# A hybrid decoder layer on one core: the last block's up groups regrouped, background sums queued later, one weight kept at each turn of halves

## The chip, the cores and the metric

The kernel runs on one core of a Trainium2 chip. The metric is the device time of one execution in microseconds (us). Five engines work beside each other: TensorE (PE, matrix products; PEld is its weight load), VectorE (DVE, elementwise work), ScalarE (ACT, activations and copies), GpSimd (POOL; here small copies and the issue of stores) and SyncE (SP; here the issue of loads and of the last stores). Each engine takes its own instructions in program order, and waits on semaphores for what others produce.

## The reference

One layer of a decoder in fp32, model width D = 1024, feed-forward width F = 2816, over 2048 prompt positions behind 16 meta tokens, and 8 sample sequences of 8 positions with cached states. Cut to what matters here:

```python
h = rmsnorm(x, norm1_g)
z = h @ w_in                                  # D -> 5D: za, zg, zp, gate_a, gate_b
a = za * sigmoid(zg)
a = causal_dwconv(a, prev_conv, conv_dw)      # width 31, per channel
conv = swish(layernorm(a + conv_b)) @ w_conv_out
pool = multiscale_pool(zp) @ w_pool * pool_scale
x = x + (sigmoid(gate_a) * conv + sigmoid(gate_b) * pool) @ w_out
u = rmsnorm(x, norm2_g) @ w_up                # D -> 2F
u = causal_dwconv(u, prev_ffn, ffn_dw)        # width 3
x = x + (gelu(gate half of u) * value half of u) @ w_down
y = rmsnorm(x, final_g)
```

The outputs are y for prompt and samples, and the new states of the three convolution and pooling branches.

## The kernel before, in words

**Data.** Channels lie on the 128 partitions, positions on the columns. The 2116 columns are worked in three blocks of 704, 704 and 708 (the last one holds the samples). An activation of one block is eight tiles (KC = 8 channel groups) of up to 708 columns; F is 22 tiles (FC). A block's columns are two halves, `FIRST` and `SECOND`, one for each of the two banks of a PSUM tile; there are four such tiles.

**Products.** Every operand is split in a high and a low part (ScalarE copies the high part, VectorE subtracts, L196 and L181), and a product of tiles is three matmuls (`gemm`, L355; the matmul itself is L222). A weight is loaded raw and split at its first use, and its two parts are stored in DRAM (`keep`); later uses load both parts (`wb<-keep`). There are four buffers for split weights and two for raw ones.

**Units.** The work of TensorE is a list of units, written out ahead for all three blocks: a unit is the products of one output tile with its weight, and behind it a post, the work on VectorE and ScalarE that takes the result out of PSUM. `WO` (L1289) is the output projection with the residual add, `FF` (L1342) the feed-forward part, `DN` (L1323) the down projection of one group of F tiles, added into x. `join` mixes the products of several units: they then go one channel tile at a time. Blocks 0 and 2 run `WO` in halves (all eight output tiles for the first half of the columns, then for the second), so that the norm of the first half can run beside the products of the second.

**Feed-forward groups.** In blocks 0 and 1 the 22 F tiles go in groups of 6, 5, 5, 6, in block 2 (`MIXED`) of 6, 6, 5, 5 (`MIX_GROUPS`). A group's down projection follows behind the first up unit of the next group. In block 2 F tiles from 3 on come from `pair` (L991): a value and a gate tile together by a scheme with seven products in place of eight. There x1, the residual, is stored to DRAM behind each group's down projection (`spill`) and loaded ahead of the next (`fetch`), to make room. The last group's down projection runs in halves in block 2, and its first three units are joined (`JOIN`).

**Background tasks.** Norms, the convolution of width 31 (`conv_norm`, L621, thirty taps for each channel tile on VectorE), the first norm of the next block (`norm1_rstd`) and the output norm (`final`, L1109) are generators. They are dripped in between the units: the planner (`Pace`, L72) holds an estimated time for each engine, and as long as VectorE's estimate lies behind TensorE's, `drip` (L1468) steps the first task whose wait is over. A task says what it waits for with `yield at(tile)` (L376), the estimated time at which that tile is ready. So the estimates alone set the order of instructions on every engine; on the chip only semaphores count.

**Sums over channels** need TensorE. `rsums` (L379) is a matmul with a matrix of ones over the accumulator of the convolution's outputs. `rstd_ps` (L387) sums squares by VectorE and ScalarE (`sumsq`), queues matmuls with a column of ones (L400, `ps<-ones,s` in the profile), works out the reciprocal root on VectorE in ten small instructions (`rs` tiles), and spreads it over the partitions with matmuls against an identity (L416, `ps<-cst,rs`). If such a matmul is queued before its accumulator is done, TensorE stands until it is.

**Weights ahead.** `w_loads` (L299) keeps up to LEAD = 4 weights in flight, counted from the oldest unit's; `w_ahead` and `split_upto` set when the raw ones are split. SyncE issues these loads in order, and x loads, fetches and the last block's y stores with them.

Of the kernel before, what the change touches and what calls it, by code (L numbers as in the profile page):

```python
# [14 lines left out]
P = 128  # L15
D = 1024
KC = D // P
F = 2816
FC = F // P
# [32 lines left out]
W_BUFS = 4  # L52
RAW_BUFS = 2
PLAIN = 3
MIX_GROUPS = (6, 6, 5, 5)
MIX_ROOM = 4
F_GROUPS = (6, 5, 5, 6)
LEAD = 4
# [2 lines left out]
AHEAD = 4  # L61
RESERVE = 3
SLACK = 200.0
JOIN = 3
OWN = 4
POOL_ORDER = (1, 0, 3, 2)
MIXED = (NBLK - 1,)
# [66 lines left out]
def trunk(ctx: ExitStack, tc: tile.TileContext, A, O):  # L134
# [238 lines left out]
        return [(o + t * h, o + (t + 1) * h + halo) for t in ts_]  # L373


    def at(ap):  # L376
        return "at", pace.ready(ap)

    def rsums(acc, n):  # L379

# [3 lines left out]
            mm(ps[:, t, : n // k], ones, acc[:, t * (n // k) : (t + 1) * (n // k)], True, True, 4.0)  # L384
        return ps[:, :k, : n // k]

    def rstd_ps(src, n):  # L387

        acc = yield from sumsq(src, n)
        yield at(acc)
        halves = 1 if n <= 512 else 2
        h = n // halves
        cuts = [(t, c) for t in range(halves) for c in [*range(0, h - P + 1, P)] + [h - P] * (h % P > 0)]
        k = len(cuts)
        ps = PSUM()
        for j, (t, c) in enumerate(cuts):
            mm(ps[:, 0, j : j + 1], acc[:, t * h + c : t * h + c + P], ones[:, :1], True, True, 260.0)  # L400
        del acc
        yield at(ps)
        w = mpool.tile([P, 4, 6], F32, tag="rs", name=nm("rs"), bufs=3)
        v, r, m, q = (w[:, i, :k] for i in range(4))
        ts(v, ps[:, 0, :k], EPS, None, ALU.add)
        ts(r.bitcast(I32), v.bitcast(I32), -0.5, MAGIC, ALU.mult, ALU.add)
        tt(m, r, r, ALU.mult)
        stt(m, m, -1.0, v, ALU.mult, ALU.mult)
        ts(q, m, 0.375, 1.25, ALU.mult, ALU.add)
        tt(q, q, m, ALU.mult)  # L410
        stt(r, q, 1.875, r, ALU.add, ALU.mult)
        tt(m, r, r, ALU.mult)
        stt(m, m, -0.5, v, ALU.mult, ALU.mult)
        stt(r, m, 1.5, r, ALU.add, ALU.mult)
        for j, (t, c) in enumerate(cuts):
            mm(ps[:, t, c : c + P], w[:, 1, j : j + 1].to_broadcast([P, P]), cst[:, O_ID : O_ID + P], True, True, 4.0)  # L416
        yield at(ps)
        return ps[:, :halves, :h]

    def rstd_of(src, n):  # L420
        ps = yield from rstd_ps(src, n)
        yield from room(1)
        out = S(n)
        act(wide(out, ps), ps, AF.Copy)
        yield at(out)
        return out
# [68 lines left out]
    def norm1_rstd(b):  # L495
        W = WIDTHS[b]
        yield from room(3)
        xs = [x_load(b, c) for c in range(2)]

        def src(c):  # L500
            x = xs.pop(0)
            if c + 2 < KC:
                xs.append(x_load(b, c + 2))
            yield at(x)
            return x

        R["rstd1", b] = yield from rstd_of(src, W)

    def h_make(b, last):
        while ("rstd1", b) not in R:  # L510
# [110 lines left out]
    def conv_norm(b):  # L621

        W = WIDTHS[b]

        def sums(c):
            if c % 2 == 0:
                yield from conv_pair(b, c)
            yield
            return R["cv", b, c]

        acc = None
        for c in range(KC):
            cv = yield from sums(c)
            if c == 1:
                yield from room(1)
                acc = S(W)
                tt(acc, R["cv", b, 0], cv, ALU.add)
            elif c:
                tt(acc, acc, cv, ALU.add)
        yield at(acc)  # L640
        ps = rsums(acc, W)
        del acc
        yield at(ps)
        yield from room(1)
        mu = S(W)
        act(mu.rearrange("p (a c) -> p a c", a=2), ps, AF.Copy)

        def src(c):
            if c == 0:
                yield at(mu)  # L650
            cv = R["cv", b, c]
            tt(cv, cv, mu, ALU.subtract)
            yield
            return cv

        ps = yield from rstd_ps(src, W)
        for c in range(KC):
            cv = wide(R["cv", b, c], ps)
            tt(cv, cv, ps, ALU.mult)
            R["cvn", b] = c + 1  # L660
            yield
# [127 lines left out]
    def add_post(b, c, ts_, ps, key):  # L789
        x = R["x1", b, c]  # L790
        yield at(x)
        tt(sb(x, b, ts_), sb(x, b, ts_), ps_of(ps, b, ts_), ALU.add)
        if key:
            for t in ts_:
                R[key, b, t] = c + 1
        yield

    def x_part(b, ts_, key):
        c0, c1 = cols(b, ts_)

        def src(c):
            ok = lambda: all(R.get((key, b, t), 0) > c for t in ts_)
            while not ok():
                yield "cond", ok
            x = R["x1", b, c][:, c0:c1]
            yield at(x)
            return x

        return src
# [298 lines left out]

    def final(b, ts_):  # L1109
        c0, c1 = cols(b, ts_)  # L1110
        r = yield from (rstd_ps if b == NBLK - 1 and ts_[-1] == 1 else rstd_of)(x_part(b, ts_, "x2n"), c1 - c0)
        for c in range(KC):
            x = R["x1", b, c][:, c0:c1]
            o = wide(x, r) if len(r.shape) == 3 else x
# [28 lines left out]
    def W(key, src, n=None):  # L1143
        wq.append(Weight(key, src, n or src.shape[1]))
        return len(wq) - 1
# [142 lines left out]

    def WO(b, parts):  # L1289
        mark["WO", b] = len(units)  # L1290
        for ts_ in parts:
            for c in range(KC):
                std_unit(
                    W(("out", c), A["w_out"][c]), lambda: R["m", b], b, ts_,
                    lambda ps, c=c, ts_=ts_: add_post(b, c, ts_, ps, "x1n"), (), wait=c == 0,
                    pre=(lambda c=c: x_again(b, c)) if ts_ == parts[0] else None,
                    drop=("m", b) if ts_ == parts[-1] and c == KC - 1 else None,
                )
                if c == 1 and ts_ == FIRST:
                    join(mark["WO", b])  # L1300
# [21 lines left out]

    def DN(b, f0, f1, parts=(BOTH,)):  # L1323
        first = len(units)
        for ts_ in parts:
            for c in range(KC):
                def after(ps, c=c, ts_=ts_):
                    yield from add_post(b, c, ts_, ps, "x2n" if f1 == FC else None)
                    if f1 < FC and b in MIXED:
                        spill(b, c)  # L1330
                    if c == KC - 1 and ts_[-1] == 1:
                        for f in range(f0, f1):
                            del R["f", b, f]

                std_unit(
                    W(("dn", c, f0, f1), A["w_dn"][c][:, f0 * P : f1 * P]), lambda: [R["f", b, f] for f in range(f0, f1)],
                    b, ts_, after, (), c == 0, pre=(lambda c=c: fetch(b, c)) if b in MIXED and ts_[0] == 0 else None,
                )
                if f1 == FC and c + 1 == JOIN and ts_ == parts[0]:
                    join(first)  # L1340

    def FF(b, parts, last_parts):  # L1342
# [11 lines left out]
        for gs in MIX_GROUPS if b in MIXED else F_GROUPS:  # L1354
            for f in range(f0, f0 + gs):
                if b in MIXED and f >= PLAIN:
                    pair(b, f)
                else:
                    if f > 1:
                        up(b, f, w_up(f), nd + ((("mx", b),) if b in MIXED and f == PLAIN - 1 else ()))  # L1360
                    if f:
                        up(b, FC + f, w_up(FC + f), nd)
                if f == f0 and pend:
                    DN(b, *pend)
                    pend = None
            pend = (f0, f0 + gs)
# [259 lines left out]
```

## Time and profile before

| what | value |
| --- | --- |
| median of 3 runs (lowest to highest) | 2970.05 us (2966.85 to 2970.11) |
| the profiled execution | 2964.97 us, of which the span of the trace 2963.1 us |
| TensorE busy | 2913.6 us, 98% |
| VectorE busy | 2034.2 us, 69% |
| ScalarE, GpSimd busy | 818.3 us (28%), 393.9 us (13%) |
| mean granted clock of TensorE | 0.992 |
| DMA | 660.13 MB, mean 223 GB/s |

In the rows of the profile, a line of the waits view gives who waits for what, the total in us, how often, and the longest; a line of the timeline gives the start, the length, the engine, line and operation with out<-in, the count, and in brackets the idle time just before it and what ended it. In the window rows "(x...)" counts instructions and PEclk is the mean granted clock over the stretch.

### The profile page before, as it was taken

The numbers are of one execution on the slowest core, as the hardware profiler recorded it, in microseconds if no ns is written. First come the engines' busy times: TensorE is split into PE (matmuls) and PEld (weight loads), VectorE is DVE, ScalarE is ACT, GpSimd is POOL, SyncE is SP. The second block draws the span as 40 slices with busy tenths as digits, with TensorE's granted clock in tenths as the row PEclk, the third lists the DMA queues.
The fourth block names the chain that finished last, engine by engine and source line by source line (L and its number), as shares of the span: only waits on it lengthen the run. The fifth ranks groups of instructions, "written<-read, shape, count | busy, mean of one in ns | idle before, by whom it ended". The sixth has DMA issues, their size and how long they took to land.

```text
span 2963.1 us, 44420 instructions
## 1 busy us (share of the span) xinstructions
PE 2913.6 (98%) x17928; PEld 2906.4 (98%) x17928; DVE 2034.2 (69%) x3007; ACT 818.3 (28%) x1238; POOL 393.9 (13%) x752
## 2 busy tenths in 40 slices
PE   7999999999999999999999999999999999999997
PEld 7999999999999999999999999999999999999997
DVE  7998998679997454743498999655672136544645
ACT  5201334333223232522221212223252113221322
POOL 1111210020010101232110000233320010000000
PEclk9999999999999999999999999999999999999999
DMA  7424554955655655798644344799964375788786
GB/s 278 157 83 163 200 204 169 343 211 176 233 178 201 215 209 189 262 337 292 247 153 150 132 139 144 266 317 320 349 230 150 131 277 185 266 281 272 269 292 241
DMA packets 156780, 660.13 MB, mean 223 GB/s; under 512 B 24992, under 2 KB 31264, under 8 KB 114720
## 3 DMA queue, kind: packets, MB, share of 16 engines
q1 hardware_dynamic: 104112, 416.19, 41.6%
q0 software_dynamic: 52464, 241.11, 20.6%
q8 instruction: 141, 2.31, 0.3%
q14 instruction: 63, 0.52, 0.1%
HBM read 433.17 MB, written 224.05 MB: 222 GB/s over the span
## 4 chain that ended last, share of the span: by engine, by line
PE 71%; DVE 12%; issue 10%; DMA 3%; POOL 2%; ACT 1%; SPq 0%; DVEq 0%; POOLq 0%; ACTq 0%
PE ps L222 71%; DVE s L185 7%; DVE s L181 3%; DVE wb L181 2%; POOL keep L216 2%; DMA wb<-keep 1%; DMA raw<-in_w_up 1%; DMA keep<-s 1%; ACT s L196 1%; DMA keep<-wb 0%; ACT wb L196 0%; POOL raw L210 0%; DMA s<-in_x 0%; SPq L205 0%; DVE rs L185 0%
## 5 line engine op out<-in xcount | busy, mean ns | idle before, releaser
L222 PE MATMUL ps<-s,wb 128*128 128x354 f32 (+3 forms) x17628 | 2879.2, 325 | 18.9 <-ACT s L196 7.6
L222 PEld LDWEIGHTS ps<-s,wb 128*128 128x128 f32 x17628 | 2867.0, 189 | 23.8 <-ACT s L196 8.7
L185 DVE SCALAR_TENSOR_TENSOR s<-s,half,s 128x704 f32<-128x704 f32 (+1 forms) x720 | 619.3, 922 | 0.0
L196 ACT ACTIVATE s<-s 128x704 fp32r<-128x704 f32 (+10 forms) x447 | 313.4, 711 | 765.5 <-DVE s L185 470.2
L181 DVE TENSOR_TENSOR s<-s,s 128x704 fp32r<-128x704 f32 (+11 forms) x526 | 401.1, 775 | 126.2 <-ACT s L196 117.3
L181 DVE TENSOR_TENSOR s<-s,ps 128x704 f32<-128x704 f32 (+4 forms) x225 | 158.4, 715 | 254.0 <-PE ps L222 208.5
L196 ACT ACTIVATE s<-ps 128x356 f32<-128x356 f32 (+6 forms) x197 | 117.3, 601 | 694.3 <-PE ps L222 677.6
L185 DVE SCALAR_TENSOR_TENSOR s<-ps,cst,s 128x704 f32<-128x704 f32 (+1 forms) x188 | 178.2, 949 | 75.8 <-ACT s L196 72.0
L216 POOL DMA_DIRECT2D keep<-s x266 | 142.8, 541 | 563.2 <-ACT s L196 460.8
L185 DVE SCALAR_TENSOR_TENSOR s<-s,cst,s 128x708 f32<-128x708 f32 (+4 forms) x188 | 156.0, 842 | 64.2 <-ACT s L196 58.0
L181 DVE TENSOR_TENSOR wb<-raw,wb 128x1024 fp32r<-128x1024 f32 (+3 forms) x136 | 152.7, 1125 | 39.0 <-ACT wb L196 38.5
L196 ACT ACTIVATE wb<-raw 128x1024 fp32r<-128x1024 f32 (+3 forms) x136 | 132.2, 977 | 155.7 <-PE ps L222 83.7
L216 POOL DMA_DIRECT2D keep<-wb x136 | 77.1, 567 | 700.0 <-DVE wb L181 683.7
L181 DVE TENSOR_TENSOR s<-raw,s 128x512 fp32r<-128x512 f32 x114 | 75.2, 687 | 107.9 <-ACT s L196 89.2
L196 ACT ACTIVATE s<-ps,cst 128x704 f32<-128x704 f32 (+1 forms) x94 | 78.9, 841 | 244.6 <-PE ps L222 235.8
L185 DVE SCALAR_TENSOR_TENSOR s<-s,ps 128x704 f32<-128x704 f32 (+6 forms) x66 | 43.8, 684 | 128.7 <-PE ps L222 117.3
L185 DVE SCALAR_TENSOR_TENSOR s<-s,s 128x704 f32<-128x704 f32 (+2 forms) x96 | 84.8, 886 | 46.2 <-ACT s L196 44.4
L196 ACT ACTIVATE s<-raw 128x512 fp32r<-128x512 f32 x114 | 68.4, 625 | 145.4 <-DMA raw<-in_w_up 122.9
L181 DVE TENSOR_TENSOR s<-s 128x718 f32<-128x718 f32 (+6 forms) x64 | 55.1, 861 | 38.3 <-ACT s L196 32.5
L216 POOL DMA_DIRECT2D out_ffn_s<-sf x44 | 23.6, 537 | 304.4 <-ACT sf L196 257.6
L185 DVE SCALAR_TENSOR_TENSOR sc<-sa,cst,sc 128x64 f32<-128x64 f32 x232 | 47.0, 279 | 1.0 <-ACT sc L196 0.7
L196 ACT ACTIVATE s<-s,half 128x704 f32<-128x704 f32 (+1 forms) x48 | 46.4, 972 | 0.8
(62 smaller groups left out, 480.9 us busy)
## 6 DMA issues: line engine op xcount, KB each, us to landing
wb<-keep SPq DMA_DIRECT2D x227, 1024.0 KB, 4.9
keep<-wb POOLq DMA_DIRECT2D x100, 1024.0 KB, 6.3
keep<-s POOLq DMA_DIRECT2D x266, 256.0 KB, 5.3
wb<-keep SPq DMA_DIRECT2D x40, 640.0 KB, 4.9
wb<-keep SPq DMA_DIRECT2D x32, 768.0 KB, 4.8
raw<-in_w_up SPq DMA_DIRECT2D x44, 512.0 KB, 4.1
raw<-in_w_in SPq DMA_DIRECT2D x40, 512.0 KB, 4.9
raw<-in_w_up POOLq DMA_DIRECT2D x38, 512.0 KB, 8.3
```

Source lines behind the costliest of these rows:

```text
L181: nc.vector.tensor_tensor(out=out, in0=a, in1=b, op=op)
L185: nc.vector.scalar_tensor_tensor(out=out, in0=a, scalar=s, in1=b, op0=op0, op1=op1)
L196: nc.scalar.activation(out, a, func, **kw)
L216: (nc.sync if last else nc.gpsimd).dma_start(out=dst, in_=src)
L222: nc.tensor.matmul(out, lhsT=lhsT, rhs=rhs, start=start, stop=stop, skip_group_check=again)
```

## The change

- `MIX_GROUPS` becomes (6, 6, 4, 3, 3) in block 2. The fourth group's down projection (F tiles 16 to 18) no longer follows the first up unit of the last group but stands behind its last one, the seven products of F tile 21. Behind it comes the last group's (F tiles 19 to 21), in halves. Between the two x1 stays where it is: no spill behind the fourth, no fetch ahead of the fifth. The first three units of the last group are no longer joined in block 2.
- `CALM` = 2500 (ns) is added to the estimated time at which a background sum's tile is ready: in `norm1_rstd` for blocks 1 and 2, in `conv_norm` for blocks 1 and 2, in `final` for blocks 0 and 1. With it, `rstd_ps` also waits for the estimate ahead of its matmuls with the identity.
- `TURN` = 1: in the second half, `WO` and `DN` take the output tiles in the order 7, 0, 1, ..., 6 and use output tile 7's weight that is still in its buffer. The keys of the residual adds become sets, since they no longer come in rising order.

```diff
@@ -52,7 +52,7 @@
 W_BUFS = 4
 RAW_BUFS = 2
 PLAIN = 3
-MIX_GROUPS = (6, 6, 5, 5)
+MIX_GROUPS = (6, 6, 4, 3, 3)
 MIX_ROOM = 4
 F_GROUPS = (6, 5, 5, 6)
 LEAD = 4
@@ -61,7 +61,9 @@
 AHEAD = 4
 RESERVE = 3
 SLACK = 200.0
+CALM = 2500.0
 JOIN = 3
+TURN = 1
 OWN = 4
 POOL_ORDER = (1, 0, 3, 2)
 MIXED = (NBLK - 1,)
@@ -373,8 +375,8 @@
         return [(o + t * h, o + (t + 1) * h + halo) for t in ts_]
 
 
-    def at(ap):
-        return "at", pace.ready(ap)
+    def at(ap, late=0.0):
+        return "at", pace.ready(ap) + late
 
     def rsums(acc, n):
 
@@ -384,13 +386,13 @@
             mm(ps[:, t, : n // k], ones, acc[:, t * (n // k) : (t + 1) * (n // k)], True, True, 4.0)
         return ps[:, :k, : n // k]
 
-    def rstd_ps(src, n):
+    def rstd_ps(src, n, late=0.0):
 
 
 
 
         acc = yield from sumsq(src, n)
-        yield at(acc)
+        yield at(acc, late)
         halves = 1 if n <= 512 else 2
         h = n // halves
         cuts = [(t, c) for t in range(halves) for c in [*range(0, h - P + 1, P)] + [h - P] * (h % P > 0)]
@@ -399,7 +401,7 @@
         for j, (t, c) in enumerate(cuts):
             mm(ps[:, 0, j : j + 1], acc[:, t * h + c : t * h + c + P], ones[:, :1], True, True, 260.0)
         del acc
-        yield at(ps)
+        yield at(ps, late)
         w = mpool.tile([P, 4, 6], F32, tag="rs", name=nm("rs"), bufs=3)
         v, r, m, q = (w[:, i, :k] for i in range(4))
         ts(v, ps[:, 0, :k], EPS, None, ALU.add)
@@ -412,13 +414,15 @@
         tt(m, r, r, ALU.mult)
         stt(m, m, -0.5, v, ALU.mult, ALU.mult)
         stt(r, m, 1.5, r, ALU.add, ALU.mult)
+        if late:
+            yield at(r, late)
         for j, (t, c) in enumerate(cuts):
             mm(ps[:, t, c : c + P], w[:, 1, j : j + 1].to_broadcast([P, P]), cst[:, O_ID : O_ID + P], True, True, 4.0)
         yield at(ps)
         return ps[:, :halves, :h]
 
-    def rstd_of(src, n):
-        ps = yield from rstd_ps(src, n)
+    def rstd_of(src, n, late=0.0):
+        ps = yield from rstd_ps(src, n, late)
         yield from room(1)
         out = S(n)
         act(wide(out, ps), ps, AF.Copy)
@@ -504,7 +508,7 @@
             yield at(x)
             return x
 
-        R["rstd1", b] = yield from rstd_of(src, W)
+        R["rstd1", b] = yield from rstd_of(src, W, CALM)
 
     def h_make(b, last):
         while ("rstd1", b) not in R:
@@ -637,7 +641,8 @@
                 tt(acc, R["cv", b, 0], cv, ALU.add)
             elif c:
                 tt(acc, acc, cv, ALU.add)
-        yield at(acc)
+        late = CALM if b else 0.0
+        yield at(acc, late)
         ps = rsums(acc, W)
         del acc
         yield at(ps)
@@ -653,7 +658,7 @@
             yield
             return cv
 
-        ps = yield from rstd_ps(src, W)
+        ps = yield from rstd_ps(src, W, late)
         for c in range(KC):
             cv = wide(R["cv", b, c], ps)
             tt(cv, cv, ps, ALU.mult)
@@ -792,14 +797,18 @@
         tt(sb(x, b, ts_), sb(x, b, ts_), ps_of(ps, b, ts_), ALU.add)
         if key:
             for t in ts_:
-                R[key, b, t] = c + 1
+                R.setdefault((key, b, t), set()).add(c)
         yield
+
+    def order_of(ts_):
+        return [*range(KC - 1, KC - 1 - TURN, -1), *range(KC - TURN)] if ts_ == SECOND else list(range(KC))
 
     def x_part(b, ts_, key):
         c0, c1 = cols(b, ts_)
 
-        def src(c):
-            ok = lambda: all(R.get((key, b, t), 0) > c for t in ts_)
+        def src(k):
+            c = order_of(ts_)[k]
+            ok = lambda: all(c in R.get((key, b, t), ()) for t in ts_)
             while not ok():
                 yield "cond", ok
             x = R["x1", b, c][:, c0:c1]
@@ -1108,7 +1117,8 @@
 
     def final(b, ts_):
         c0, c1 = cols(b, ts_)
-        r = yield from (rstd_ps if b == NBLK - 1 and ts_[-1] == 1 else rstd_of)(x_part(b, ts_, "x2n"), c1 - c0)
+        last = b == NBLK - 1 and ts_[-1] == 1
+        r = yield from (rstd_ps if last else rstd_of)(x_part(b, ts_, "x2n"), c1 - c0, 0.0 if b == NBLK - 1 else CALM)
         for c in range(KC):
             x = R["x1", b, c][:, c0:c1]
             o = wide(x, r) if len(r.shape) == 3 else x
@@ -1288,13 +1298,16 @@
 
     def WO(b, parts):
         mark["WO", b] = len(units)
+        ws = {}
         for ts_ in parts:
-            for c in range(KC):
+            for c in order_of(ts_):
+                if ts_ != SECOND or c < KC - TURN:
+                    ws[c] = W(("out", c), A["w_out"][c])
                 std_unit(
-                    W(("out", c), A["w_out"][c]), lambda: R["m", b], b, ts_,
-                    lambda ps, c=c, ts_=ts_: add_post(b, c, ts_, ps, "x1n"), (), wait=c == 0,
+                    ws[c], lambda: R["m", b], b, ts_,
+                    lambda ps, c=c, ts_=ts_: add_post(b, c, ts_, ps, "x1n"), (), wait=c == order_of(ts_)[0],
                     pre=(lambda c=c: x_again(b, c)) if ts_ == parts[0] else None,
-                    drop=("m", b) if ts_ == parts[-1] and c == KC - 1 else None,
+                    drop=("m", b) if ts_ == parts[-1] and c == order_of(ts_)[-1] else None,
                 )
                 if c == 1 and ts_ == FIRST:
                     join(mark["WO", b])
@@ -1322,21 +1335,24 @@
 
     def DN(b, f0, f1, parts=(BOTH,)):
         first = len(units)
+        ws = {}
         for ts_ in parts:
-            for c in range(KC):
+            for c in order_of(ts_):
+                if ts_ != SECOND or c < KC - TURN:
+                    ws[c] = W(("dn", c, f0, f1), A["w_dn"][c][:, f0 * P : f1 * P])
                 def after(ps, c=c, ts_=ts_):
                     yield from add_post(b, c, ts_, ps, "x2n" if f1 == FC else None)
-                    if f1 < FC and b in MIXED:
+                    if f1 < FC - MIX_GROUPS[-1] and b in MIXED:
                         spill(b, c)
-                    if c == KC - 1 and ts_[-1] == 1:
+                    if c == order_of(ts_)[-1] and ts_[-1] == 1:
                         for f in range(f0, f1):
                             del R["f", b, f]
 
                 std_unit(
-                    W(("dn", c, f0, f1), A["w_dn"][c][:, f0 * P : f1 * P]), lambda: [R["f", b, f] for f in range(f0, f1)],
-                    b, ts_, after, (), c == 0, pre=(lambda c=c: fetch(b, c)) if b in MIXED and ts_[0] == 0 else None,
+                    ws[c], lambda: [R["f", b, f] for f in range(f0, f1)],
+                    b, ts_, after, (), c == order_of(ts_)[0], pre=(lambda c=c: fetch(b, c)) if b in MIXED and ts_[0] == 0 and f1 < FC else None,
                 )
-                if f1 == FC and c + 1 == JOIN and ts_ == parts[0]:
+                if f1 == FC and c + 1 == JOIN and ts_ == parts[0] and b not in MIXED:
                     join(first)
 
     def FF(b, parts, last_parts):
@@ -1360,7 +1376,7 @@
                         up(b, f, w_up(f), nd + ((("mx", b),) if b in MIXED and f == PLAIN - 1 else ()))
                     if f:
                         up(b, FC + f, w_up(FC + f), nd)
-                if f == f0 and pend:
+                if f == (f0 if f0 + gs < FC or b not in MIXED else FC - 1) and pend:
                     DN(b, *pend)
                     pend = None
             pend = (f0, f0 + gs)
```

## The prediction

> **What bounds the kernel now.** I read the page first, then TensorE's waits, then TensorE's timeline and a table of windows around each wait. The page's head and the totals of TensorE's waits:
>
> ```profile
> span 2963.1 us, 44420 instructions
> PE 2913.6 (98%) x17928; PEld 2906.4 (98%) x17928; DVE 2034.2 (69%) x3007; ACT 818.3 (28%) x1238; POOL 393.9 (13%) x752
> PE ps L222 <- DVE s L181: 18.0, 6, 9.9
> PE ps L222 <- ACT s L196: 7.6, 4, 2.3
> PE ps L222 <- DVE rs L185: 6.6, 4, 2.0
> PE ps L222 <- DMA wb<-keep: 5.0, 5, 2.5
> PE ps L222 <- issue: 3.8, 1, 3.8
> ```
>
> TensorE is busy for 98% of the span, and the change leaves its number of products alone. So all that can be won is idle time of TensorE: 41 us in these rows, of which the start-up takes the one wait of 9.9. The rest is a handful of places. Next, windows of TensorE: length, busy time and count of matmuls, granted clock (mean of the stretch), DMA share, GB/s. The first is an undisturbed stretch; the others hold one wait each.
>
> ```profile
> core 0: us, PE busy (x), PEclk, DMA share, GB/s
> 1000.00:1100.00 100.00, 100.00 (x618) 1.00 0.67 234
> 612.00:636.00 24.00, 20.48 (x108) 0.86 0.30 108
> 886.00:902.00 16.00, 11.28 (x52) 0.79 0.82 295
> 1632.00:1643.00 11.00, 7.24 (x36) 0.84 0.28 101
> 2455.00:2469.00 14.00, 11.06 (x52) 0.76 0.49 189
> 2902.00:2919.00 17.00, 12.59 (x66) 0.90 0.62 223
> ```
>
> An undisturbed matmul takes 100/618 = 0.162 us. A wait costs more than its idle time: in each of the five other rows the clock falls below 1. I charge a wait with its idle time plus busy time times (1 - clock). That gives 3.5 + 2.9 = 6.4 us at 612 (place C), 4.7 + 2.4 = 7.1 at 886 (place D), 3.8 + 1.2 = 5.0 at 1632 (E) and 2.9 + 2.7 = 5.6 at 2455 (G). At 2902 (H) it gives 4.4 + 1.3 = 5.7; the count there gives 17.0 - 66 x 0.162 = 6.3, and since this window holds only products of one kind, I take the count.
>
> **Place D: the sums of the second block's convolution.** Here `conv_norm(1)` queues two matmuls with `ones` on TensorE behind the seventh down product of a group. TensorE's and VectorE's timelines (start, length, instruction, idle time before it and its releaser):
>
> ```profile
> 892.12 2.68 PE L222 MATMUL ps<-s,ones 128*128 128x352 f32 x4 [4.72 <-DVE s L181]
> 890.16 1.81 DVE L181 TENSOR_TENSOR s<-s,s 128x704 f32<-128x704 f32 x2
> ```
>
> VectorE finishes the accumulator at 891.97 and TensorE starts 0.15 later. CALM queues the two matmuls later. TensorE's order at this place, before (weights wb_7708 and wb_7749 are the down blocks 6 and 7 of that group):
>
> ```order
> L222 MATMUL ps_7843<-s_7510,wb_7708 128x352
> L222 MATMUL ps_7843<-s_7509,wb_7708 128x352
> L222 MATMUL ps_7885<-s_4224,ones 128x352 x2
> L222 MATMUL ps_7889<-s_6515,wb_7749 128x352
> L222 MATMUL ps_7889<-s_6516,wb_7749 128x352
> ```
>
> And now (wb_7785 is the weight of the up unit that follows those eight down blocks):
>
> ```order
> L224 MATMUL ps_7922<-s_5492,wb_7785 128x354 x2
> L224 MATMUL ps_7922<-s_5493,wb_7785 128x354
> L224 MATMUL ps_7922<-s_5492,wb_7785 128x354
> L224 MATMUL ps_7979<-s_4224,ones 128x352 x2
> L224 MATMUL ps_7985<-s_5272,wb_7827 128x354
> ```
>
> The 30 products of down block 7 and the 48 of the up unit now stand ahead: 78 x 0.162 = 12.6 us against 4.72 of wait. The 7.1 us go, with 7.9 us to spare. The other background sums (rstd1 of block 1, y of blocks 0 and 1) move by a unit or more as well; none has a wait in the rows above, so they are worth nothing. E is a wait on a product's PSUM slot, whose order is the same in both: 0.
>
> **Place C: turn to the first up products of block 0.** TensorE's timeline:
>
> ```profile
> 612.63 9.53 PE L222 MATMUL ps<-s,wb 128*128 128x354 f32 x57 [0.85 <-DVE wb L181]
> 621.99 0.72 PE L222 MATMUL ps<-ones,s 128*128 128x1 f32 x6
> 622.58 1.70 PE L222 MATMUL ps<-s,wb 128*128 128x354 f32 x9
> 624.76 0.93 PE L222 MATMUL ps<-cst,rs 128*128 128x128 f32 x6 [0.47 <-DVE rs L185]
> 627.50 0.66 PE L222 MATMUL ps<-s,wb 128*128 128x354 f32 x1 [1.81 <-ACT s L196]
> ```
>
> The second half's `cst` matmuls are the last before products that need the second half's rows, so all of the normalization (2.74 us from 624.76 to 627.50) stands open. TURN keeps output block 7's weight, and the second half begins with that block: one load fewer, so the planner's window of four weights reaches the up weights one unit sooner. It splits them on VectorE sooner, and the sums follow sooner. VectorE's order right behind the rstd chain, before:
>
> ```order
> L185 SCALAR_TENSOR_TENSOR rs_5595<-rs_5595 128x3 x2
> L185 SCALAR_TENSOR_TENSOR s_4300<-s_2481,half,s_4300 128x704
> L185 SCALAR_TENSOR_TENSOR s_4287<-s_2343,half,s_4287 128x704
> L185 SCALAR_TENSOR_TENSOR s_5613<-s_4882,cst,s_5611 128x352
> L185 SCALAR_TENSOR_TENSOR s_5616<-s_4884,cst,s_5611 128x352
> ```
>
> And now:
>
> ```order
> L187 SCALAR_TENSOR_TENSOR rs_5575<-rs_5575 128x3 x2
> L187 SCALAR_TENSOR_TENSOR s_5600<-s_4882,cst,s_5598 128x352
> L187 SCALAR_TENSOR_TENSOR s_5612<-s_4884,cst,s_5598 128x352
> L183 TENSOR_TENSOR s_5273<-s_5600,s_5272 128x352
> L187 SCALAR_TENSOR_TENSOR s_5616<-s_4886,cst,s_5598 128x352
> ```
>
> Two convolution taps (the rows with `half`) no longer stand ahead of the normalization. On TensorE the `ones` matmuls stand behind 45 of the group's 72 products and `cst` behind 54, where before it was 63 and 72. So 18 products, 2.9 us, now cover the 2.74. What stays is the 0.47 ahead of `cst`, which still has nine products of cover. Gain 6.4 - 0.5 = 5.9; between 3.0 (the idle alone, less 0.5) and 6.4.
>
> **Place H: the last products.** TensorE's timeline at the end of the seven-product units:
>
> ```profile
> 2904.74 5.10 PE L222 MATMUL ps<-s,wb 128*128 128x354 f32 x30 [1.59 <-DMA wb<-keep]
> 2912.16 0.43 PE L222 MATMUL ps<-s,wb 128*128 128x354 f32 x1 [2.32 <-ACT s L196]
> 2913.09 22.59 PE L222 MATMUL ps<-s,wb 128*128 128x354 f32 x128 [0.51 <-DVE s L181]
> ```
>
> Pair 21 ends at 2903.15 and its result is complete at 2913.09, 9.9 us later; the joined last down units have only 36 products (5.8 us) without it. Now DN(16,19) stands between: 8 units of 18 products = 144 x 0.162 = 23.3 us. Both waits on f = 21 go. The wait of 1.59 for the first weight doesn't go by itself; that weight has 384 KB instead of 640, so I leave 0.5 of it. Gain 5.8, between 3.8 (idle alone) and 6.3. The extra down group adds eight adds on VectorE, which is idle for 31% of the span: 0. No extra spill or fetch is made, since x1 stays in place between the fourth group and the fifth.
>
> **Place G: block 2's first up products** wait for weights that share the queues with spills:
>
> ```profile
> 2459.57 3.17 PE L222 MATMUL ps<-s,wb 128*128 128x356 f32 x12 [2.54 <-DMA wb<-keep]
> wb<-keep SPq DMA_DIRECT2D x5, 1024.0 KB, 8.0
> xd<-s POOLq DMA_DIRECT2D x6, 354.0 KB, 7.3
> ```
>
> (The last two are issues between 2440 and 2468: count, KB each, median us to landing.) With the order 7, 0 to 6 one spill of 354 KB falls behind this place. At the 295 GB/s of the row at 886 it is worth 1.2 us. Ends 0 and 5.6; the row says that five loads and six spills compete, so I stay near 0: 1.2.
>
> **The new tail.** The last group has three blocks, so a unit has 9 products and 384 KB instead of 15 and 640. TensorE, then VectorE, then medians of loads of three sizes (the first and last over the kernel):
>
> ```profile
> 2935.52 0.72 PE L222 MATMUL ps<-ones,s 128*128 128x1 f32 x6
> 2936.10 2.67 PE L222 MATMUL ps<-s,wb 128*128 128x354 f32 x15
> 2938.62 0.83 PE L222 MATMUL ps<-cst,rs 128*128 128x128 f32 x6
> 2950.99 0.80 PE L222 MATMUL ps<-ones,s 128*128 128x1 f32 x6 [1.80 <-DVE s L181]
> 2953.82 1.65 PE L222 MATMUL ps<-cst,rs 128*128 128x128 f32 x6 [2.04 <-DVE rs L185]
> 2949.66 1.18 DVE L181 TENSOR_TENSOR s<-s,s 128x354 f32<-128x354 f32 x2
> wb<-keep SPq DMA_DIRECT2D x40, 640.0 KB, 4.9
> raw<-in_w_dn SPq DMA_DIRECT2D x16, 384.0 KB, 3.6
> ```
>
> - *First half's cst.* Uncovered, `ones` to `cst` takes 2953.82 - 2950.99 = 2.83 us; 0.58 of it is `ones` itself, and one unit of 9 products now covers 1.46 instead of 2.4. Cost 0.8.
> - *Last sums.* Behind the last add VectorE now has five sums queued where it had two (1.18 us): three more at 0.44 to 0.63, so 1.3 to 1.9; I take 1.5.
> - *Weights.* Four buffers mean that a load has three units, 27 x 0.162 = 4.37 us. At 3.6 us it is hidden; at 4.9 each round of four units waits 0.53, over 16 units 2.1. I take 0.6. SyncE's last rows now, where keep_6705 and keep_6754 are the last two weights:
>
> ```order
> L207 DMA wb_26303<-keep_6655 128x2x384
> L207 DMA wb_26332<-keep_6705 128x2x384
> L218 DMA out_y<-s_25943 128x354
> L207 DMA wb_26351<-keep_6754 128x2x384
> L218 DMA out_y<-s_25966 128x354
> ```
>
> Before, all weight loads stood ahead of the first store. The last load now waits in SyncE's queue until VectorE has scaled the first y tile; it is part of the 0.6.
>
> Tail: 0.8 + 1.5 + 0.6 = +2.9, between 1.3 and 4.8.
>
> **Sum.** -7.1 - 5.9 - 5.8 - 1.2 + 2.9 = -17.1 us. The profiled execution took 2964.97 us, 5.1 under the median of the runs; against it that is 2947.9, against the median 2970.05 it is 2953.0.
>
> **A rule against the rows.** The windows at 612 and 2902 lose clock after idle stretches of 1.8 to 2.5 us. The Trainium skill (TensorE: Matmul & The Clock Gate, "What's actually happening") has the clock halved only after an idle window of about 3.4 us. By that rule alone C and H would be worth their idle time: -7.1 - 3.0 - 3.8 - 1.2 + 2.9 = -12.2, 2957.8. The trace disagrees for these places (0.86 and 0.90 there), so I keep the larger terms.
>
> **The rivals.**
>
> 1. *VectorE bounds block 1.* The window between the two places (TensorE, weight loads, VectorE, ScalarE, GpSimd busy), and the weight split with the least reserve, which ends at 865.58 for products at 867.89:
>
> ```profile
> 643.00:892.00 249.00, 244.40 (x1507) 244.12 (x1505) 242.61 (x276) 74.95 (x91) 22.59 (x38) 1.00 0.59 206
> 864.76 0.82 DVE L181 TENSOR_TENSOR wb<-raw,wb 128x640 fp32r<-128x640 f32 x1
> ```
>
> VectorE is busy for 97% of it. If C brings TensorE forward by 5.9 and VectorE only by the two taps (1.8), the reserve of 2.3 is short by 1.8 us; if it comes forward by nothing, by 3.6. With half clock as in the rows above (2.4 more) it gives back 4.2 to 6.0, say 5.2: 2958. Against it: VectorE's work also starts earlier after C. Chance 0.15.
>
> 2. *The sums' wait only moves.* If VectorE's convolution ends later against the products (it fills the idle time with other tasks first), D's 7.1 stays: 2960. Against it stands the reserve of 7.9 us. Chance 0.07. With rival 1 together: 2965.
>
> 3. *Slower: the tail runs at the pace of its loads.* If 384 KB take L, a round of four units waits L - 4.37, and gaps of 2 us bring half clock to about half of the 23 us: 4 x (L - 4.37) + 11.7. From L = 5.9 it eats the whole gain; at the 8.0 of the row in place G it is 26.2, so 2970.05 - 17.7 + 26.2 = 2978.6. For it: loads that compete took 8.0. Against it: those have 1024 KB, no fetch or spill runs beside the last 16 units, and 384 KB took 3.6. Chance 0.04.
>
> 4. *Clock as in the rule above*: 2957.8. Chance 0.05.
>
> **How the numbers follow.** My forecast has 0.65; 0.04 is left for a wait at a place that I don't see, as likely up as level. The best ends give -7.1 - 6.4 - 6.3 - 5.6 + 1.3 = -24.1, 2946; the worst ends give -4.7 - 3.0 - 3.8 + 4.8 = -6.7, 2963; rivals 1 and 2 together reach 2965. Range 2946 to 2965. A difference of 0.2% (5.9 us) is about what a measurement of this kernel can tell from none: faster means under 2964.1. That takes in the forecast and rivals 1, 2 and 4, less their unlucky ends: 0.86; same 0.09; slower 0.05.
>
> **What would show it.** Right: no idle row ahead of `ps<-s,ones` in block 1; clock 1.00 from 612 to 640; no wait on ACT or DVE ahead of the last down units; one new row of 0.5 to 1 us ahead of the first half's `cst` in the tail, and about 3.3 us ahead of the last `ones`. Wrong: a new row `<-DVE wb L181` of over 1 us between 850 and 890, several rows `<-DMA wb<-keep` in the last 25 us, or clock below 1 at a place that was at 1.

## The result and the profile after

| | before | changed |
| --- | --- | --- |
| median (lowest to highest) | 2970.08 us (2966.85 to 2970.25, 4 runs) | 2947.21 us (2944.55 to 2952.47, 4 runs) |
| profiled execution | 2964.97 us | 2945.39 us |

The ratio is 0.9928, with an interval of 0.9911 to 0.9945: 21 us faster, between 16 and 26. A second set of runs gave 2947.59 against 2968.01, 0.9942 (0.9929 to 0.9955), 13 to 21 us faster. Forecast were 2953.0 and a gain of 17.1; the profiled executions differ by 19.6.

The page's head of the changed kernel and the totals of TensorE's waits (lines are two higher than before: L224 is the matmul, L183 VectorE's tensor_tensor):

```profile
span 2943.6 us, 44436 instructions
PE 2902.4 (99%) x17928; PEld 2895.6 (98%) x17928; DVE 2040.3 (69%) x3015; ACT 817.5 (28%) x1238; POOL 388.2 (13%) x752
PE ps L224 <- DVE s L183: 14.4, 3, 10.1
PE ps L224 <- DVE rs L187: 7.5, 6, 2.0
PE ps L224 <- DMA wb<-keep: 4.1, 3, 2.5
PE ps L224 <- issue: 3.9, 1, 3.9
PE ps L224 <- ACT s L198: 3.6, 2, 1.9
PE ps L224 <- DVE wb L183: 0.5, 2, 0.3
```

The waits add up to 34.0 us where they were 41.9: only 7.9 of the 19.5 us of span are idle time. The rest stands in the busy time: 2902.4 for 2913.6 with the same 17928 matmul records, 11.2 us less. More than half of this pair's gain is matmuls that no longer run at half clock behind a wait. A narrow window behind the wait at H in the kernel before shows the clock at half (length, busy time and count, granted clock, DMA share, GB/s):

```profile
2914.40:2917.60 3.20, 3.20 (x13) 0.50 0.78 232
```

Not all of these 11.2 us are the change's doing. A window's length times (1 - clock) is the time that it loses by the clock. At the start-up (34 to 50 us) the clock was 0.68 before and is 0.79 now, at place G 0.76 and 0.88: 1.8 and 1.7 us less lost, behind waits that are still there. I put these 3.5 us down to the two executions and not to the change: over 34 to 50 us, experiment 8, with the same start-up, has 0.68 again.

The same windows as in the prediction, shifted with the work: places C, D, E, G and H.

```profile
600.00:624.00 24.00, 23.52 (x149) 1.00 0.68 261
884.00:900.00 16.00, 16.00 (x97) 1.00 0.94 316
1616.00:1627.00 11.00, 7.14 (x35) 0.84 0.30 118
2440.00:2454.00 14.00, 10.51 (x56) 0.88 0.56 228
2884.00:2901.00 17.00, 16.97 (x105) 1.00 0.80 259
```

D and H are full, C is full but for 0.48 us, and all three are at clock 1.00. E is unchanged. G still has its wait of 2.54 us and a new one of 0.46 ahead of `cst`, and a higher clock. TensorE's timeline at C, at D, and from pair 21 to the end:

```profile
618.82 1.70 PE L224 MATMUL ps<-s,wb 128*128 128x354 f32 x9
620.99 0.93 PE L224 MATMUL ps<-cst,rs 128*128 128x128 f32 x6 [0.48 <-DVE rs L187]
621.68 18.61 PE L224 MATMUL ps<-s,wb 128*128 128x354 f32 x113
...
892.66 1.35 PE L224 MATMUL ps<-s,ones 128*128 128x352 f32 x4
...
2889.70 27.38 PE L224 MATMUL ps<-s,wb 128*128 128x354 f32 x164
2916.92 0.72 PE L224 MATMUL ps<-ones,s 128*128 128x1 f32 x6
2917.51 1.71 PE L224 MATMUL ps<-s,wb 128*128 128x354 f32 x9
2919.68 0.93 PE L224 MATMUL ps<-cst,rs 128*128 128x128 f32 x6 [0.46 <-DVE rs L187]
2920.38 7.78 PE L224 MATMUL ps<-s,wb 128*128 128x354 f32 x45
2931.84 0.80 PE L224 MATMUL ps<-ones,s 128*128 128x1 f32 x6 [3.68 <-DVE s L183]
```

From pair 21 on TensorE runs 27 us without a stop, where before it stood three times. The tail shows a new wait of 0.46 ahead of the first half's `cst`, and the one ahead of the last `ones` has grown from 1.80 to 3.68. VectorE's timeline says why:

```profile
2928.20 0.52 DVE L183 TENSOR_TENSOR s<-s,ps 128x354 f32<-128x354 f32 x1 [0.73 <-PE ps L224]
2928.63 3.06 DVE L183 TENSOR_TENSOR s<-s,s 128x354 f32<-128x354 f32 x5
```

Five sums, 3.06 us, stand behind the last add, where two took 1.18.

### The profile page after: what moved, and what is told of

It is laid out like the page before. It is cut to its first block, busy times and chain, and to the rows that moved or that the text cites. A ratio compares the mean times of both kernels' runs of the same rounds, so it can differ in the third digit from the quotient of the medians.

```text
span 2943.6 us, 44436 instructions
## 1 busy us (share of the span) xinstructions
PE 2902.4 (99%) x17928; PEld 2895.6 (98%) x17928; DVE 2040.3 (69%) x3015; ACT 817.5 (28%) x1238; POOL 388.2 (13%) x752
## 4 chain that ended last, share of the span: by engine, by line
PE 86%; issue 4%; DVE 4%; DMA 3%; ACT 1%; POOL 1%; SPq 0%; DVEq 0%; POOLq 0%; ACTq 0%
PE ps L224 86%; DVE s L187 2%; POOL keep L218 1%; DMA raw<-in_w_out 1%; DVE s L183 1%; ACT s L198 1%; DVE wb L183 1%; DMA wb<-keep 1%; DMA keep<-s 1%; ACT wb L198 0%; DMA raw<-in_w_in 0%; SPq L207 0%; DMA cst<-in_cst 0%; DMA raw<-in_w_up 0%; POOL raw L212 0%
## 5 line engine op out<-in xcount | busy, mean ns | idle before, releaser
L224 PE MATMUL ps<-s,wb 128*128 128x354 f32 (+3 forms) x17628 | 2870.5, 325 | 12.6 <-DMA wb<-keep 4.1
L224 PEld LDWEIGHTS ps<-s,wb 128*128 128x128 f32 x17628 | 2858.3, 189 | 17.1 <-issue 8.7
L183 DVE TENSOR_TENSOR s<-s,s 128x704 fp32r<-128x704 f32 (+11 forms) x526 | 401.1, 775 | 123.4 <-ACT s L198 115.0
L183 DVE TENSOR_TENSOR s<-s,ps 128x704 f32<-128x704 f32 (+4 forms) x233 | 165.2, 720 | 251.8 <-PE ps L224 210.8
L183 DVE TENSOR_TENSOR wb<-raw,wb 128x1024 fp32r<-128x1024 f32 (+3 forms) x136 | 152.7, 1125 | 42.5 <-ACT wb L198 41.9
L183 DVE TENSOR_TENSOR s<-raw,s 128x512 fp32r<-128x512 f32 x114 | 75.1, 686 | 95.6 <-ACT s L198 63.6
L183 DVE TENSOR_TENSOR s<-s 128x718 f32<-128x718 f32 (+6 forms) x64 | 55.0, 859 | 29.8 <-ACT s L198 22.5
```

The lines of the kernel that those rows point to most:

```text
L183: nc.vector.tensor_tensor(out=out, in0=a, in1=b, op=op)
L224: nc.tensor.matmul(out, lhsT=lhsT, rhs=rhs, start=start, stop=stop, skip_group_check=again)
```

## The experiments

Experiments 1 to 4 share one set of runs of the kernel before, with a median of 2966.87 us; 5 to 8 share a second (2968.01), 9 to 12 a third (2969.24). The ratio beside a time is worked out from all runs of both kernels, with its 95% interval in brackets, so it differs a little from the ratio of the medians.

**1. CALM alone.** Edit, against the changed kernel; the conditions on the last group are those of before again:

```diff
-MIX_GROUPS = (6, 6, 4, 3, 3)
+MIX_GROUPS = (6, 6, 5, 5)
-TURN = 1
+TURN = 0
```

> CALM alone on the kernel before (groups 6 6 5 5, no kept weight). In TensorE's order the sums of the second block's convolution now stand 30 products later (behind down block 7), not 78: 4.9 us against the wait of 4.72. Theory (the prediction's place D, carried by CALM): the wait and its slow clock go almost wholly, -7 us, 2963; the rows at 611 to 634, at 2455 and after 2902 stay. Rival (VectorE is full there and only fills the time with other work first): the same wait of 4 to 5 us stands 5 us later, 0 us, 2970.

2957.88 us, 0.9968 (0.9958 to 0.9979), 6 to 12 us faster. TensorE's row at place D, and one at place G:

```profile
893.90 1.37 PE L224 MATMUL ps<-s,ones 128*128 128x352 f32 x4
...
2453.76 2.20 PE L224 MATMUL ps<-s,wb 128*128 128x356 f32 x12 [2.59 <-DMA wb<-keep]
```

The first has no idle time, so 30 products of cover are just enough for the wait of 4.72. VectorE's being full there did not move the wait; the rival falls. The second shows G's wait without slow clock: 12 matmuls in 2.20 us, where they took 3.17 before and 3.67 in the changed kernel, each behind 2.54 us.

**2. The kept weight alone.** `TURN = 1`, `CALM = 0`, groups as before.

> The kept weight alone (TURN = 1, CALM = 0, groups 6 6 5 5). Theory: it shortens place C (611 to 634) by 6 to 7 us, and since its order of TensorE also puts the convolution's sums of the second block behind the next up unit, 65 rows later, with no CALM at all, it takes place D too: -14 us in all, 2956, no idle row ahead of the matmuls with ones in block 1. Rival (the prediction's bookkeeping, in which only CALM removes D): -7 us, 2963, with D's wait of about 4.7 us still there.

2953.43 us, 0.9952 (0.9939 to 0.9965). TensorE's timeline at C and D:

```profile
619.98 0.93 PE L224 MATMUL ps<-cst,rs 128*128 128x128 f32 x6 [0.48 <-DVE rs L187]
620.66 9.64 PE L224 MATMUL ps<-s,wb 128*128 128x354 f32 x58
...
892.27 1.35 PE L224 MATMUL ps<-s,ones 128*128 128x352 f32 x4
```

At C only the 0.48 is left, and D's wait is gone, without any CALM. The kept weight moves the second block's sums as far as the whole change does: in TensorE's order they stand at the same place with and without CALM, 78 products later than before (30 with CALM alone).

**3. The groups alone.** `CALM = 0`, `TURN = 0`.

> The groups 6 6 4 3 3 with the late down projection alone (CALM = 0, TURN = 0). Theory: the waits after pair 21 (6.3 to 6.7 us) go, the tail costs 2.9: -3.5 us, 2966.5; C and D stay at 6 to 7 us each. Rival (the tail runs at the pace of its loads): rows of waits on wb<-keep in the last 25 us, no gain, 2970 or more.

2966.76 us, 1.0 (0.9991 to 1.0008). C and D stay, as they should. Pair 21 to the end, TensorE's timeline:

```profile
2889.75 46.03 PE L224 MATMUL ps<-s,wb 128*128 128x356 f32 x277
...
2938.38 0.93 PE L224 MATMUL ps<-cst,rs 128*128 128x128 f32 x6 [0.50 <-DVE rs L187]
...
2950.68 1.21 PE L224 MATMUL ps<-ones,s 128*128 128x1 f32 x6 [3.68 <-DVE s L183]
```

The waits behind pair 21 are gone, and none of TensorE's rows there waits for a weight: the tail doesn't run at the pace of its loads. But the expected 3.5 us did not come. Its profiled execution lost time at a place in block 1 where the order of instructions is the same as before, row for row, on every engine. TensorE there, and ScalarE ahead of it; then ScalarE in the kernel before:

```profile
1973.03 12.23 PE L224 MATMUL ps<-s,wb 128*128 128x352 f32 x75 [2.77 <-ACT s L198]
1965.46 1.15 ACT L198 ACTIVATE s<-raw 128x512 fp32r<-128x512 f32 x2 [6.42 <-DMA raw<-in_w_up]
```

```profile
1958.49 1.16 ACT L196 ACTIVATE s<-raw 128x512 fp32r<-128x512 f32 x2 [4.66 <-DMA raw<-in_w_up]
```

TensorE starts the same products at 1958.7 in both, but the raw weight that GpSimd's queue loads for the seven-product weights came 7.0 us later in the one. The copy of that weight stands at the head of ScalarE's queue, its split at the head of VectorE's, with the posts that free PSUM behind them. Most of the 7.0 us was there before the load began: GpSimd issued it 5.2 us later (this experiment, then the kernel before), and ScalarE had already got the pair of raw weights ahead of it 5.2 us later.

```profile
1956.89 0.55 POOL L212 DMA_DIRECT2D raw<-in_w_up  x1
...
1951.68 1.09 POOL L210 DMA_DIRECT2D raw<-in_w_up  x2
```

So the lag built up over several loads, and where it began is open. This is one execution. It can't tell why the median of eleven runs didn't fall; that stays open too.

**4 and 5. The changed kernel without CALM, and the changed kernel again.** `CALM = 0`; and no edit.

> The changed kernel without CALM (CALM = 0, everything else as changed). Theory (the kept weight alone already moves the second block's sums far enough): as fast as the whole change within 1.5 us, ratio about 0.992 to 0.994, 2949. Rival (CALM carries place D): 7 us slower than the changed kernel, about 2955, with an idle row of 4 to 5 us ahead of the matmuls with ones.

> The changed kernel again, beside the three below. Theory A (CALM adds nothing that shows, since the kept weight moved the second block's sums): as fast as without CALM, ratio 0.9935 to 0.995. Theory B (CALM is worth 5 us more on top): 0.992 to 0.993. In the trace of both the same waits are expected: the turn at about 618 (0.5 us), about 1617 (3.8), about 2441 (3), the last sums (3.7).

2950.83 us, 0.9945 (0.9933 to 0.9958), and 2947.59 us, 0.9942 (0.9929 to 0.9955). Theory A holds: CALM adds nothing that shows on top of the kept weight. The 3 us between the medians are not settled. Experiment 4's profile has the late raw weight again, 4.16 us of idle time at 1959, and the two sets of runs of the changed kernel differ by as much in their ratios (0.9928 and 0.9942). Against experiment 2 the groups bring 2.6 us by the medians, but the intervals overlap: what they buy isn't shown by a time.

**6. Sums ahead of the scaling in the tail.**

```diff
-        for ts_ in SPLIT if b == NBLK - 1 else (BOTH,):
+        for ts_ in SPLIT[::-1] if b == NBLK - 1 else (BOTH,):
             add_task(("y", b, ts_), final(b, ts_), ...)
```

> The changed kernel with the two output norms of the last block taken in the other order by the planner, so that the second half's sums of squares stand ahead of the first half's scaling on VectorE; behind the last add stand two sums instead of five. Theory (the tail's cost is the queue on VectorE): the wait ahead of the last matmuls with ones falls from 3.7 to about 2.0 us, the time by 1.5 to 2.5. Rival (the last products wait for their weights, or the scaling only moves behind the last norm): the wait stays or the end comes as late, 0.

2947.74 us, 0.994 (0.9928 to 0.9953). The wait did fall, by 1.4 us, TensorE:

```profile
2933.50 0.80 PE L224 MATMUL ps<-ones,s 128*128 128x1 f32 x6 [2.27 <-DVE s L183]
```

So the queue on VectorE is the wait's cause. The end comes earlier with it: from the end of the last product to the last instruction it is 14.1 us, where experiment 5's profile has 15.4. The time doesn't show it: 1.4 us is less than the runs scatter.

**7. A truer estimate for the late raw weights**, in `load_later`:

```diff
-        pace.put("pool", 600.0, [out], [], late=2000.0 + move)
+        pace.put("pool", 600.0, [out], [], late=8000.0 + move)
```

> The changed kernel with one number changed: the planner takes 8 us instead of 2 for a raw weight that GpSimd's queue loads for the seven-product weights (its median to landing in the page is 8.3 us). Theory: the wait of 3 to 6 us that stood at about 1955 to 1970 in two of four executions, with the same order of instructions as in one that didn't show it, comes from such a load landing late while VectorE and ScalarE have its split at the head of their queues; it goes for good, the median falls by 1 to 4 us and the runs scatter less. Rival (the wait comes from another source, or the split only moves): same median and scatter.

2946.71 us (2945.63 to 2948.26), 0.9935 (0.9923 to 0.9948). The median fell by 0.9 us, which is inside the intervals. The five runs lie within 2.6 us, where those of the changed kernel lay within 6.6 and, earlier, 7.9. That speaks for the theory, but no profile caught the wait going: this one doesn't have it, and neither have the two of the changed kernel.

**8. Taps held back in block 1.**

```diff
+        quiet = quiet or mark["FF", 1] <= now["i"] < mark["FF", 1] + 3
```

> The changed kernel, in which background convolution taps are held back during the first three up units of block 1's feed-forward part. Theory for place E (up unit 231 waits for the PSUM slot of unit 227, whose post stands behind 19 taps on VectorE): the row of 3.8 us at about 1617 and its slow clock go, -5 us, if the taps held back don't delay the sums of the last block's convolution, which now stand 100 rows later. Rival: the taps make TensorE wait there, 0 or slower.

2958.11 us, 0.9973 (0.9964 to 0.9983): 10 us slower than the changed kernel. TensorE twice, then ScalarE ahead of the first:

```profile
1622.45 12.79 PE L224 MATMUL ps<-s,wb 128*128 128x354 f32 x63 [5.18 <-issue]
1852.62 2.70 PE L224 MATMUL ps<-s,ones 128*128 128x354 f32 x4 [6.35 <-DVE s L183]
...
1612.06 1.15 ACT L198 ACTIVATE s<-raw 128x512 fp32r<-128x512 f32 x2 [11.00 <-DMA raw<-in_w_up]
```

The row at E didn't go. The planner filled the free time on VectorE with weight splits instead of taps, and these waited for a raw weight (11.00 us on ScalarE, 9.98 on VectorE behind it), so something still stood ahead of the post. The rival came too: the convolution that was held back made TensorE wait at its sums.

**9. Five tiles in the last group, still with the late group.** `MIX_GROUPS = (6, 6, 5, 5)` in the changed kernel.

> The changed kernel with groups 6 6 5 5 in place of 6 6 4 3 3; the late down projection (now of F tiles 12 to 16), the resident x1, the kept weight and CALM stay. Theory (the late group takes the waits at 2902 to 2918 away, and the small last group is what costs the tail 3 us): units of 15 products cover the first half's cst again and VectorE no longer falls behind; no row ahead of that cst, about 1.8 us ahead of the last ones; 2 to 3 us faster than the changed kernel, ratio 0.9925 to 0.9935. Rival (the tail's cost comes with the kept weight's order or with the late group itself): the same 3.7 us ahead of the last ones, 0.

2946.08 us, 0.9925 (0.9913 to 0.9937), 23.2 us under the kernel before by the medians of its set (20.4 for the changed kernel in its own). The intervals overlap, so the time doesn't show a gain; the waits do. TensorE's tail:

```profile
2911.24 0.83 PE L224 MATMUL ps<-cst,rs 128*128 128x128 f32 x6
...
2925.22 2.68 PE L224 MATMUL ps<-s,wb 128*128 128x354 f32 x15 [0.95 <-DMA wb<-keep]
2929.70 0.98 PE L224 MATMUL ps<-ones,s 128*128 128x1 f32 x6 [1.80 <-DVE s L183]
```

The first `cst` is covered again and the last wait is back at 1.80, so the small last group is what costs the tail. The late group with x1 kept in place takes H's waits away with three tiles in the last group and with five. What came in place of the tail's cost is 0.95 for a weight.

**10. Two tiles in the last group.** `MIX_GROUPS = (6, 6, 4, 4, 2)`.

> The changed kernel with groups 6 6 4 4 2: the last units have 6 products, 0.97 us, and 256 KB. Theory (the prediction's third rival decides once a load takes longer than three units): three units are 2.9 us; the 384 KB loads of the tail took 4.1, so with 3.3 to 4 us for 256 KB a round of four units waits 0.4 to 1.1, with slow clock 3 to 10 us slower than the changed kernel, in rows that wait on wb<-keep. Rival: VectorE's adds (0.52 us each, and a sum or a scaling beside each) are slower than 0.97 us and the rows wait on DVE: 2 to 5 us slower. If neither shows, 0 to 2.

2950.89 us, 0.9948 (0.9934 to 0.9962). TensorE's waits for weights and VectorE in the tail:

```profile
2913.88 1.22 PE L224 MATMUL ps<-s,wb 128*128 128x354 f32 x6 [0.27 <-DMA wb<-keep]
2915.34 3.26 PE L224 MATMUL ps<-s,wb 128*128 128x354 f32 x18 [0.24 <-DMA wb<-keep]
2918.78 4.10 PE L224 MATMUL ps<-s,wb 128*128 128x354 f32 x24 [0.19 <-DMA wb<-keep]
2923.54 1.22 PE L224 MATMUL ps<-s,wb 128*128 128x354 f32 x6 [0.65 <-DVE s L183]
...
2936.64 1.44 PE L224 MATMUL ps<-ones,s 128*128 128x1 f32 x6 [5.44 <-DVE s L183]
```

The loads did take longer than three units (median 3.3 us against 2.9) and cost 0.7 us in three rows. VectorE costs far more: it ends 5.44 us behind the last product. The rival's way of slowing down is the one that came.

**11. A reserve on VectorE at place E**, in `drip`:

```diff
-        while free["dve"] < free["pe"] - SLACK:
+        slack = 6000.0 if mark["FF", 1] <= now["i"] < mark["FF", 1] + 3 else SLACK
+        while free["dve"] < free["pe"] - slack:
```

> The changed kernel in which the planner leaves 6 us instead of 0.2 between VectorE's and TensorE's estimate during the first three up units of block 1: fewer taps (about 13 for 19) stand ahead of those units' posts, the order of TensorE stays word for word. Theory for place E (up unit 231 waits for a PSUM slot whose post stands behind background work on VectorE): the row of 3.8 us at about 1617 and its slow clock go, -4 to -5.5 us against the changed kernel, ratio 0.992. Rival (the wait is not of the posts' queue): it stays, 0.

2946.13 us, 0.9926 (0.9914 to 0.9938). TensorE at E, and at two places where the changed kernel had a smaller wait or none:

```profile
1604.77 20.39 PE L224 MATMUL ps<-s,wb 128*128 128x354 f32 x125
...
1845.82 1.47 PE L224 MATMUL ps<-ones,s 128*128 128x1 f32 x12 [2.40 <-DVE s L183]
...
2078.55 6.74 PE L224 MATMUL ps<-s,wb 128*128 128x352 f32 x31 [2.49 <-DMA wb<-keep]
```

E is gone, so it was background work ahead of the post: 12 taps stand right ahead of it now, 19 in the changed kernel. About as much came back: 2.40 at the last block's convolution norm, whose taps now end later, and 2.49 for a weight. The second need not be the edit's: in the two profiles of the changed kernel that wait was 1.05 and 0.62. The gain on the changed kernel is inside the intervals.

**12. The edits of 6, 7 and 11 together.**

> The changed kernel with three edits together: 6 us of reserve in block 1's first up units, 8 us as the estimate for raw weights on GpSimd's queue, and the second half's sums of squares ahead of the first half's scaling. Theory: their effects add up: -5 (place E), -1 (late raw weights), -1.4 (tail) against the changed kernel: about 2940, ratio 0.990 to 0.992, and runs within 4 us. Rival: only place E counts, 0.9925.

2940.77 us (2939.96 to 2941.01), 0.9906 (0.9893 to 0.9919): the fastest, as expected, and its four runs lie within 1.1 us. The head of its page, and the place where the reserve gives part of its gain back:

```profile
span 2938.2 us, 44430 instructions
...
1845.49 1.47 PE L224 MATMUL ps<-ones,s 128*128 128x1 f32 x12 [2.34 <-DVE s L183]
```

That the three effects add up is not shown: one by one the edits moved the medians by less than the runs scatter. Against experiment 11 this profile lacks the 2.49 for a weight with the slow clock behind it, and the last `ones` wait 2.28 for 3.68.

## Why the prediction was right, step by step

The time lies in the range and the gain is of the forecast size. The steps, by the profiled executions:

- **C, -5.9: right.** The row of 0.48 ahead of `cst` stayed and everything behind it went; clock 1.00. Experiment 2 shows that the kept weight does it. That the planner's window of four weights is the reason is read from the code and the order, not tested.
- **D, -7.1: right in size, wrong in cause.** The step that failed is "CALM queues the two matmuls later", as the reason for the 78 products and the 7.9 us to spare. With CALM alone they stand 30 products later, 4.9 us against 4.72, with hardly any reserve; the 78 products were the kept weight's doing, and it needs no CALM (experiments 1, 2, 4). The 7.1 us came out all the same, since either part alone takes the wait away; that is luck, not the reasoning. I read the order of the whole change and put all of it down to the part whose text speaks of queuing. Why the kept weight moves a sum 270 us later is argued only: the planner put two taps behind the norm at place C, and the convolution's estimate with them.
- **H, -5.8: right in the trace**, rather 6.3; even the 0.5 left for the first weight went. The profiles of experiments 3 and 9 show it with either grouping. No time shows it: with the tail's +2.9 it should have brought 2.9 us, and the groups alone brought nothing (experiment 3, ratio 0.9991 to 1.0008).
- **G, -1.2: not shown.** The step that failed is that one spill fewer ahead of this place shortens the wait: it is 2.54 as before. Only the clock differs (0.88 for 0.76), and that differs between executions: behind 2.59 in experiment 1 and 2.92 in experiment 3 it was 1.00 throughout.
- **Tail, +2.9: right in size.** The parts were 0.8, 1.5 and 0.6. Measured were 0.46 for `cst`, 1.9 more ahead of the last `ones`, and no row that waits for a weight: 2.3 together. Experiments 6 and 9 show the causes. The lower bound of 1.3 was too low by its own parts, 0.8 and 1.3; that moves the range by 0.8 us.
- **From -17.1 to the time.** The terms came to 2947.9 for the profiled execution, which took 2945.39. I then added 5.1, by which before's median lay above its profiled execution. For the changed kernel that distance is 1.8: it is no constant, and a forecast on the median carries some 3 us of it. The two pairs of medians give gains of 23 and 20 us and ratios worth 21 and 17, so the forecast of 17.1 is as near as the runs can tell.

Of the rivals, *VectorE bounds block 1* falls: from 631 to 877 TensorE stood at no time.

```profile
631.00:877.00 246.00, 246.00 (x1522) 1.00 0.58 201
```

*The sums' wait only moves* falls by the row at 892.66. *The tail at the pace of its loads* falls by the changed kernel's own tail: its loads of 384 KB took 4.1 us in the median, more than the 3.6 I took and less than the 4.37 that three units last, and no row waits for one. Experiment 10 shows what happens past that limit. *The clock by idle windows of 3.4 us alone* (the Trainium skill, TensorE: Matmul & The Clock Gate, "What's actually happening") would have left 12.2 us. The trace disagrees: before, the windows at C and H lost clock behind idle stretches of 1.81 and 2.32 us, now they are at 1.00, and the profiled gain was 19.6. But experiments 1 and 3 show that a wait of 2.6 to 2.9 us doesn't always cost clock, so what I put for it in one trace is one draw.

## What to carry to other kernels

Where estimates set the order, read from the order of each part alone what that part moves; a part's name says little, and two parts may buy the same thing. A wait of 2 to 3 us on a busy TensorE is worth its idle time and, in these traces, 0, 1.7 or 3.4 us lost to slow clock on top, not the same in each execution. Read such a cost from more than one profile. When an engine is relieved ahead of one wait, look at who lives on that engine's next free time: experiments 8 and 11 moved a wait, and 8 paid more than it won.

## What the runs showed of the hardware

- Clock: behind idle time of 0.48 us (the row ahead of `cst` at C) the granted clock stayed 1.00; behind 2.54 and 3.86 us it fell (0.88 and 0.84 in the windows at G and E of the changed kernel). Before, 1.81 us at C and 2.32 at H already brought it to 0.86 and 0.90 over their windows.
- The slow stretches come in sizes. Length times (1 - clock) of the windows gives 1.7 us (H before, E and G now), 3.4 (C, D and G before) or 5.1 (start-up before). At half clock these are stretches of about 3.4, 6.8 and 10 us.
- The same wait doesn't always bring one: at G, 2.54 us cost 3.4 in the kernel before and 1.7 in the changed kernel, and 2.59 and 2.92 in experiments 1 and 3 cost nothing (12 matmuls in 2.20 and 2.17 us). What decides it isn't shown.
- The same instructions in the same order waited 0 or 2.77 us at one place of block 1, by whether a raw load on GpSimd's queue landed 7.0 us earlier or later; 5.2 of these had built up before it was issued. Such a wait is a candidate for the scatter of several us between runs; that the scatter shrank with the truer estimate (2.6 and 1.1 us) speaks for it, without proof.
